# Attention values from rounded high and low parts, and split q and k turned by a product with the identity

## The chip, the cores and the metric

One core of a Trainium2 chip runs the whole program. The metric is the device time of one execution in microseconds, the median over three runs. The engines are TensorE (PE, with its weight loads listed apart as PEld), VectorE (DVE), ScalarE (ACT), GpSimd (POOL) and SyncE (SP), which here issues the DMAs.

## What is computed

One decoder layer over 1024 tokens behind 16 learned meta tokens, all in float32: RMS norm, one input projection, three groups of heads that read the same normalised input (stick-breaking attention, a Mamba-2 state-space group, HGRN2), an output projection, and a squared-ReLU MLP. The change lies in the attention group, 4 heads of 64. Cut to what matters:

```
z = einsum('qd,kd->qk', q, k) * scale           # q, k: RMS-normalised per head
log_w = log_sigmoid(z) + (suffix sum of log_sigmoid(-z) over the keys behind k)
w = where(k < q, exp(log_w), 0)                 # the weights of one block of 128 queries
o = einsum('qk,kd->qd', w, v)                   # the values
out = rmsnorm(o, out_norm)                      # per head
```

## The kernel before

A tile is 128 tokens; tile 0 is the 16 meta tokens, tiles 1 to 8 the sequence. The program goes through these stages: a norm and transposes of the input; `in_gemm` (L366), which projects every tile onto the attention values v (256 columns) and eight decay logits; attention; then eight chunks of state-space and HGRN2 work with the output projection; then the MLP.

Large products are made of float32 numbers split in two: a high part rounded to the type that TensorE takes in a single pass (F32R), written by ACT, and a low part (the number less its high part), written by DVE. A product is then hi*hi + hi*lo + lo*hi, three single-pass matmuls (`gemm_steps`, L185). Plain float32 operands (F32) are also taken by TensorE: the profile then shows two weight loads and two matmuls for each matmul that the program writes.

Attention goes over tiles i = 1 to 8 and in each over heads h = 0 to 3. For each head `scores` (L624), run two heads ahead, forms z in PSUM, takes two sigmoids on ACT, and scans along the keys on DVE. `values` (L652) then takes the weights `sg` in groups of up to four blocks of 128 keys: it transposes them on PE into the one PSUM bank `pb`, copies them to SBUF on ACT (`wT`), and multiplies each block by its tile of v:

```
urgent[0] = A.copy(wT[:, 0:n], pw[:, 0:n])
fill(VGAP)
for j in grp:
    mm(po[:, h * 64:(h + 1) * 64], lhsT=wT[...], rhs=vt[j // 4][:, j % 4, h * 64:(h + 1) * 64], ...)
fill(SGAP); next(ahead, None); fill(HGAP)
```

Here `wT` and `vt` are plain float32, so each block has two loads and two matmuls of 64 columns. There are 48 groups (tiles 1 to 4 have one per head, tiles 5 to 8 two) with 144 blocks in all. After the fourth head a last product adds the meta tokens (`vmb`, L677).

PE's instructions are issued in the order in which the program writes them (`queue`, L112). The orders of DVE, ACT and POOL are made at compile time by a scheduler that simulates the engines; each of them then runs its list in order. `fill(n)` (L757) puts n matmuls of other work between: products of the state-space and HGRN2 projections (bank `mf`), or of the q and k projection of a later tile (bank `mq`). What the fillers have not done by the end of attention is done right after it (L1510), so the total of PE's work doesn't hang on these counts. Each filler product brings work of its own for ACT, DVE and POOL (a convolution of three DVE operations, `split_scaled` of the next weights, and so on).

At the start of each tile `prep_b` (L604) splits the normalised q and k of the next tile into high and low parts side by side, and `stack` (L576) transposes them with `tr`, four 128 by 128 blocks each for q and k: 68 transposes with the tile of meta tokens. At the end of each tile `head_norm` (L565) takes the 256 columns of `po` (one of two buffers of bank `pc`): square on ACT, sum on DVE, a reciprocal root on POOL, a product on DVE, and a store.

Of the kernel before, what the change touches and what calls it, by code (L numbers as in the profile page):

```python
# [8 lines left out]
F32 = mybir.dt.float32  # L9
F32R = mybir.dt.float32r  # L10
BF16 = mybir.dt.bfloat16
U8 = mybir.dt.uint8
AF = mybir.ActivationFunctionType
ALU = mybir.AluOpType

P = 128
D = 1024
# [5 lines left out]
G3 = L + 16  # L23
# [24 lines left out]
ITR = (7, 0)  # L48
PRE = (24, 16, 24, 14, 22, 28)
FILL = (0, 20, 24, 28, 16, 40, 40, 46, 46)  # L50
SGAP, HGAP, VGAP, LOADGAP, BGAP, QGAP, WGAP = 1, 6, 9, 20, 8, 3, 12

BUFS = dict(g1=4, g2=2, g3=8, wsA=1, wsB=1, k4=4, st=3, a1=1, a2=1, a3=1, a4=1, a5=1, qb=1, f4=1, wT=2,
            igt=1, rr=6, ro=2, sm=4, sst=1, fp=2)
# [3 lines left out]
def inner(ap, shape):  # L58

    return ap.rearrange("p (n o) -> p n o", o=1).broadcast_to(shape)  # L60
# [8 lines left out]
def tile_hybrid_block(  # L69
# [34 lines left out]
    V, A, G, SY = (Pinned(e) for e in (nc.vector, nc.scalar, nc.gpsimd, nc.sync))  # L104
# [7 lines left out]
    def queue(i):  # L112
        if fixed[0] and last[0] is not None:
            behind(i, last[0])
        last[0] = i
        return i

    def mm(*a, **k):
        return queue(nc.tensor.matmul(*a, **k))  # L119

    def tr(*a, **k):
        return queue(nc.tensor.transpose(*a, **k))  # L122
# [4 lines left out]
    kto = pool.tile([P, 512], F32, tag="kto", bufs=1, name="kto")  # L127
# [5 lines left out]
    def sb(shape, tag, dt=F32):  # L133
        if tag in ring:
            r = ring[tag]
            r[3] += 1
            at = r[0] + r[3] % r[1] * r[2]
            return cx[:, at:at + shape[0]]
        cnt[0] += 1
        return pool.tile([P] + list(shape), dt, tag=tag, bufs=BUFS[tag], name=f"{tag}_{cnt[0]}")  # L140

    def const(shape, name, dt=F32):
        return pool.tile([P] + list(shape), dt, tag=name, bufs=1, name=name)

    def ps(tag):
        cnt[0] += 1
        return psp.tile([P, 512], F32, tag=tag, bufs=PBUFS[tag], name=f"{tag}_{cnt[0]}")
# [27 lines left out]
    def rms_r(ss, m, n):  # L175

        G.tensor_scalar(ss[:m, :n], ss[:m, :n], 1.0, EPS, ALU.mult, ALU.add)
        rms_last[0] = G.tensor_tensor(ss[:m, :n], ss[:m, :n], mhalf[:m, :n], op=ALU.pow)
# [3 lines left out]
    def rms_tile(tag="rr"):  # L182
        return sb([8], tag)
# [24 lines left out]
    def load_x(i):  # L208
        xt = sb([G3], "g3")[:, 0:D]
        SY.dma_start(xt[:TILES[i][1]], meta if i == 0 else xf[(i - 1) * P:i * P, :])  # L210
        xts[i] = xt
# [40 lines left out]
    ident = const([P], "ident")  # L252
# [4 lines left out]
    pt = ps("pa")  # L257
# [9 lines left out]
    identr, smask = mi[:, 0], mi[:, 1]  # L267
# [85 lines left out]
    def tok_steps(dst, i, w, n0, n1):  # L353
        col, m = TILES[i]
        return gemm_steps(dst, lambda k, a: hx(k, a, col, m), lambda k, a: w[a][:, k, n0:n1])


    vmb = kto[:, 0:256]
    V.memset(vmb, 0.0)
    wv = [sb([KC, NV], t, F32R) for t in ("wsA", "wsB")]  # L360
    vt = [None, None]

    order = [1, 2, 0, 3, 4, 5, 6, 7, 8]
    wq = []
# [1 line left out]
    def in_gemm(n, i):  # L366
        m = TILES[i][1]
        pv = ps(("mq", "pc")[n % 2])
        yield from tok_steps(pv[:m, :NV], i, wv, 0, NV)
        if i:  # L370
            j = (i - 1) // 4
            if vt[j] is None:
                vt[j] = sb([G3], "g3")[:, 0:D].rearrange("p (a b) -> p a b", b=256)
            A.copy(vt[j][:, (i - 1) % 4, :], pv[:m, 0:256])
        else:
            for h in range(4):
                A.copy(vmb[32 * h:32 * h + NM, 64 * h:64 * h + 64], pv[:NM, 64 * h:64 * h + 64])
        V.tensor_copy(dtt[:m, i, :], pv[:m, 256:NV])
        if i == 1:
            load_x(8)  # L380
# [19 lines left out]
    for n, i in enumerate(order):  # L400
        g = in_gemm(n, i)
        if n + 2 < len(order):
            in_norm(order[n + 2])
        for q in range(2):
            take(g, ITR[q] if n else (18, 0)[q])
            if n + 1 < len(order):
                in_tr(order[n + 1], q)
        run(g)
        if n == 2:
            with tc.issue_after(rms_last[0].ins):  # L410
                more_constants()
                masks()
        if n >= 2:
            next(loads, None)
# [142 lines left out]
    def fq_dots():  # L557
        _, p, kg, i0, o0, ni = lateral.pop(0)
        pd = ps("pa")
        for i in range(ni):  # L560
            mm(pd[:, 2 * i:2 * i + 2], lhsT=kg[:, o0 + i * P:o0 + (i + 1) * P], rhs=blk1, start=True, stop=True)
        V.tensor_copy(dtok[:, i0:i0 + ni, p, :], pd[:, 0:2 * ni].rearrange("p (a b) -> p a b", b=2))


    def head_norm(src, m, nh, tag="a1"):  # L565

        nf = sb([8, 64], tag) if tag == "a1" else kto[:, 256:512].rearrange("p (h d) -> p h d", d=64)
        sv = src[:m, :nh * 64].rearrange("p (h d) -> p h d", d=64)
        r = rms_tile("rr" if tag == "a1" else "ro")
        A.activation(nf[:m, :nh], sv, AF.Square, scale=64 ** -0.5)  # L570
        V.reduce_sum(r[:m, :nh], nf[:m, :nh], axis=mybir.AxisListType.X)
        rms_r(r, m, nh)
        V.tensor_tensor(nf[:m, :nh], sv, inner(r[:m, :nh], [m, nh, 64]), op=ALU.mult)
        return nf

    def stack(src, m, tag, bank):  # L576

        hl = sb([4, 2, 64], tag, F32R)
        A.copy(hl[:m, :, 0, :], src)
        V.tensor_tensor(hl[:m, :, 1, :], src, hl[:m, :, 0, :], op=ALU.subtract)  # L580
        pt = ps(bank)
        hf = hl.bitcast(F32)
        for h in range(4):
            tr(pt[:, h * P:h * P + m], hf[:m, h].rearrange("p a d -> p (a d)"), ident[:m, :m])
        return pt

    kT = [sb([G3], "g3", F32R) for _ in range(4)]
# [4 lines left out]
    def prep_a(i):  # L592

        m = TILES[i][1]
        pq = ps("mq" if i else "pc")
        if i == 0:
            yield from tok_steps(pq[:m, :256], i, wq, 256, 512)
            nfs[i] = head_norm(pq, m, 4)
        else:
            yield from tok_steps(pq, i, wq, 0, 512)  # L600
            nfs[i] = head_norm(pq, m, 8)
            G.tensor_tensor(nfs[i][:, 0:4], nfs[i][:, 0:4], outer(wqk, [P, 4, 64]), op=ALU.mult)
# [49 lines left out]
    def values(i, h, po, ahead):  # L652
        sg = sgs.pop((i, h))
        for g0 in range(0, i, 4):
            grp = range(g0, min(i, g0 + 4))
            pw = ps("pb")
            for j in grp:
                tr(pw[:, (j - g0) * P:(j - g0 + 1) * P], sg[:, NM + j * P:NM + (j + 1) * P], ident)
            wT = sb([512], "wT")
            n = len(grp) * P  # L660
            urgent[0] = A.copy(wT[:, 0:n], pw[:, 0:n])
            fill(VGAP)
            for j in grp:
                mm(po[:, h * 64:(h + 1) * 64], lhsT=wT[:, (j - g0) * P:(j - g0 + 1) * P],
                   rhs=vt[j // 4][:, j % 4, h * 64:(h + 1) * 64], start=(h == 0 and j == 0), stop=False)
            fill(SGAP)
            next(ahead, None)
            fill(HGAP)
        for _ in ahead:
            fill(HGAP)  # L670
        if h == 3:
            pw = ps("pb")
            tr(pw[:, 0:P], wm[i % 2].rearrange("p h s -> p (h s)"), ident)
            wT = sb([512], "wT")
            urgent[0] = A.copy(wT[:, 0:P], pw[:, 0:P])
            fill(VGAP)
            mm(po[:, 0:256], lhsT=wT[:, 0:P], rhs=vmb, start=False, stop=True)  # L677


    def z_tile(i):  # L680
# [76 lines left out]
    def fill(n):  # L757
        budget[0] -= n
        while n and fillers:
            if next(fillers[0], True):  # L760
                fillers.pop(0)
                continue
            n -= 1
            nfill[0] += 1
            if side and nfill[0] % LOADGAP == 0 and next(side[0], True):
                side.pop(0)
            if lateral and nfill[0] - lateral[0][0] >= 40:
                fq_dots()
# [29 lines left out]
    sgs, po = {}, None  # L798
# [5 lines left out]
    for n, (i, h) in enumerate(hs):  # L804
        budget[0] = FILL[i]
        if h == 0 and i < 8:
            if i > 1:
                drain(pre[i + 1])
            prep_b(i + 1)
            if i == 7:  # L810
                side.append(load_cols(C_Z, wz))
        if h == 1 and i < 7:
            start_a(i + 2)
        if n == 30:
            side.append(load_wi())
        if h == 0:
            po = ps("pc")
        values(i, h, po, scores(*hs[n + 2]) if n + 2 < len(hs) else iter(()))
        fill(max(0, budget[0]))
        if h == 3:  # L820
            on = head_norm(po, P, 4, "ob")
            SY.dma_start(dr_o[(i - 1) * P:i * P, :], on.rearrange("p h d -> p (h d)"))
# [730 lines left out]
    for i, tag in (("s2", "g2"), ("s3", "g2"), ("22", "g1"), ("s1", "g1")):  # L1553
        t = slab(tag)
# [101 lines left out]
```

## Time and profile before

| | |
|---|---|
| median of 3 runs | 1239.97 us (1239.06 to 1240.15) |
| the profiled execution, its own time | 1240.42 us |
| its span, first to last instruction | 1238.7 us |
| busy share of the span: PE, PEld, DVE, ACT, POOL | 98%, 84%, 71%, 47%, 34% |
| matmuls, and weight loads, in the trace | 6396, 6396 |

All times are in microseconds from the start of the span, unless marked ns. A busy share of PE counts each matmul from its start to the arrival of its last result, and matmuls overlap; what a matmul costs in a stream is the distance between starts, not its duration. Attention runs from 76 to 362 us.

### The profile page before, as it was taken

How to read it: one execution, taken by the hardware profiler on the slowest of the kernel's cores; microseconds unless marked ns; L12 is line 12 of the kernel's file. 1: busy time of each engine (PE TensorE's matmuls, PEld its weight loads, DVE VectorE, ACT ScalarE, POOL GpSimd, SP SyncE). 2: the span in 40 equal slices, each digit the busy share in tenths (PEclk: the TensorE clock that was granted, in tenths of full speed). 3: DMA queues.
4: the chain of work that ended last, by engine and by line, in shares of the span. 5: the costliest groups of instructions: out<-in, count | busy, mean ns of one | idle time of the engine just before them, and what ended most of it. 6: DMA issues, size and time to landing. Idle time of an engine off the chain costs nothing.

```text
span 1238.7 us, 18662 instructions
## 1 busy us (share of the span) xinstructions
PE 1211.4 (98%) x6396; PEld 1038.2 (84%) x6396; DVE 881.1 (71%) x1451; ACT 584.4 (47%) x1237; POOL 424.6 (34%) x498
## 2 busy tenths in 40 slices
PE   8999999999999989999999999999999999999998
PEld 7989999999888768888888888888777888888887
DVE  6777777775323688888456756667998778778777
ACT  6655676664332242333356644454566534344331
POOL 4223322322111467666424646656851000000000
PEclk9999999999999999999999999999999999999999
DMA  6311111233345575462256667767766554554566
GB/s 217 89 41 46 55 40 58 72 95 101 81 125 134 159 227 133 103 128 79 85 162 190 215 210 239 238 225 256 241 212 202 165 162 140 158 158 141 162 197 206
DMA packets 195031, 184.14 MB, mean 149 GB/s; under 512 B 14405, under 2 KB 149853, under 8 KB 194938
## 3 DMA queue, kind: packets, MB, share of 16 engines
q1 hardware_dynamic: 194938, 182.97, 49.3%
q8 instruction: 50, 0.82, 0.3%
q14 instruction: 43, 0.35, 0.1%
HBM read 128.25 MB, written 54.67 MB: 148 GB/s over the span
## 4 chain that ended last, share of the span: by engine, by line
PE 81%; DVE 7%; issue 3%; ACT 3%; POOL 3%; DMA 2%; SPq 0%; DVEq 0%; POOLq 0%; ACTq 0%
PE pa L119 26%; PE mf L119 24%; PE pc L119 17%; PE mq L119 6%; PE pb L119 4%; DVE g L96 2%; DVE k L96 2%; PE pb L122 1%; POOL rr L96 1%; DVE cx L96 1%; PE pa L122 1%; DMA g<-in_w_out_dram 1%; DVE a L96 1%; PE pc L122 1%; POOL cx L96 1%
## 5 line engine op out<-in xcount | busy, mean ns | idle before, releaser
L119 PE MATMUL pa<-g,k 128*128 128x512 f32 x864 | 208.8, 389 | 0.8 <-DVE f L96 0.8
L119 PEld LDWEIGHTS pa<-g,k 128*128 128x128 f32 x864 | 162.0, 188 | 35.2 <-DVE f L96 1.2
L119 PE MATMUL mf<-g,wsA 128*128 128x384 f32 (+2 forms) x624 | 139.3, 357 | 0.0
L119 PE MATMUL mf<-g,wsB 128*128 128x384 f32 (+2 forms) x624 | 137.3, 355 | 0.0
L119 PEld LDWEIGHTS mf<-g,wsA 128*128 128x128 f32 x624 | 103.8, 190 | 6.5 <-DVE g L96 0.3
L119 PEld LDWEIGHTS mf<-g,wsB 128*128 128x128 f32 x624 | 103.4, 189 | 5.8
L96 DVE TENSOR_TENSOR k<-g,k 128x512 fp32r<-128x512 f32 x80 | 81.2, 1016 | 28.7 <-ACT k L96 28.5
L119 PE MATMUL mf<-g,g 128*128 128x512 f32 (+1 forms) x408 | 101.1, 395 | 0.0
L96 ACT CAST g<-cx 128x512 fp32r<-128x512 f32 x80 | 49.5, 619 | 85.5 <-DVE cx L96 58.9
L119 PEld LDWEIGHTS mf<-g,g 128*128 128x128 f32 (+1 forms) x408 | 72.4, 183 | 15.0 <-issue 0.3
L119 PE MATMUL pc<-g,k 128*128 128x512 f32 x336 | 82.5, 389 | 0.0
L96 DVE TENSOR_TENSOR g<-pa,g 128x512 f32<-128x512 f32 (+2 forms) x82 | 54.8, 678 | 36.6 <-PE pa L119 32.2
L96 POOL TENSOR_TENSOR cx<-cx 128x384 f32<-128x384 f32 (+2 forms) x34 | 38.5, 1134 | 118.9 <-ACT cx L96 78.6
L119 PEld LDWEIGHTS pc<-g,k 128*128 128x128 f32 x336 | 63.1, 188 | 13.2
L119 PE MATMUL mf<-g,k 128*128 128x512 f32 x288 | 69.6, 392 | 1.6 <-ACT a L96 1.3
L119 PE MATMUL pa<-g,st 128*128 128x512 f32 x240 | 65.1, 390 | 0.3 <-ACT g L96 0.3
L119 PEld LDWEIGHTS mf<-g,k 128*128 128x128 f32 x288 | 53.6, 188 | 13.4 <-ACT a L96 1.8
L96 DVE TENSOR_TENSOR g<-cx,g 128x512 fp32r<-128x512 f32 x80 | 60.5, 756 | 4.9 <-ACT g L96 3.5
L96 POOL TENSOR_TENSOR g<-g,g 128x512 f32<-128x512 f32 x32 | 45.7, 1437 | 49.8 <-issue 45.5
L96 ACT CAST k<-g 128x512 fp32r<-128x512 f32 x80 | 48.9, 615 | 17.6 <-PE pb L119 9.1
L119 PEld LDWEIGHTS pa<-g,st 128*128 128x128 f32 x240 | 45.0, 188 | 10.1 <-ACT g L96 0.8
L96 DVE SCALAR_TENSOR_TENSOR cx<-cx,cwb 128x384 f32<-128x384 f32 (+1 forms) x72 | 43.5, 605 | 9.2 <-ACT cx L96 8.6
(365 smaller groups left out, 2713.8 us busy)
## 6 DMA issues: line engine op xcount, KB each, us to landing
g<-in_w_up_dram SPq DMA_DIRECT2D x48, 512.0 KB, 4.9
st<-in_w_in_dram SPq DMA_DIRECT2D x51, 256.0 KB, 2.9
cx<-in_w_down_dram SPq DMA_DIRECT2D x48, 256.0 KB, 3.1
wT<-dr_s SPq DMA_DIRECT2D x45, 256.0 KB, 2.9
dr_s<-a SPq DMA_DIRECT2D x40, 256.0 KB, 2.3
g<-in_x_dram SPq DMA_DIRECT2D x16, 512.0 KB, 4.5
dr_s<-st SPq DMA_DIRECT2D x32, 256.0 KB, 2.4
a<-dr_s SPq DMA_DIRECT2D x23, 256.0 KB, 2.9
```

The costliest lines, as they stand in the source:

```text
L96: i = fn(*a, **k)
L119: return queue(nc.tensor.matmul(*a, **k))
L122: return queue(nc.tensor.transpose(*a, **k))
```

## The change

The values of each tile are now kept as a rounded high part and a low part, 64 columns of each side by side for every head (`vt`, four buffers where there were two, each for two tiles). The transposed weights are copied out rounded (`wT`), and a new DVE subtraction writes their low part (`wl`). For each block there is one single-pass matmul of `wT` with 128 columns (v high and v low), and, two filler matmuls later (`LGAP`), one single-pass matmul of `wl` with the 64 columns of v high. `po` holds high and low sums side by side, 128 columns for a head, and `head_norm` first copies the low half out (ACT) and adds the two (DVE). The gap behind the scores, `HGAP`, goes from 6 fillers to 4. In `stack` the transpose becomes a single-pass matmul of the split tile with a rounded identity.

```diff
--- before.py
+++ after.py
@@ -48,7 +48,7 @@
 ITR = (7, 0)
 PRE = (24, 16, 24, 14, 22, 28)
 FILL = (0, 20, 24, 28, 16, 40, 40, 46, 46)
-SGAP, HGAP, VGAP, LOADGAP, BGAP, QGAP, WGAP = 1, 6, 9, 20, 8, 3, 12
+SGAP, HGAP, VGAP, LOADGAP, BGAP, QGAP, WGAP, LGAP = 1, 4, 9, 20, 8, 3, 12, 2
 
 BUFS = dict(g1=4, g2=2, g3=8, wsA=1, wsB=1, k4=4, st=3, a1=1, a2=1, a3=1, a4=1, a5=1, qb=1, f4=1, wT=2,
             igt=1, rr=6, ro=2, sm=4, sst=1, fp=2)
@@ -358,7 +358,8 @@
     vmb = kto[:, 0:256]
     V.memset(vmb, 0.0)
     wv = [sb([KC, NV], t, F32R) for t in ("wsA", "wsB")]
-    vt = [None, None]
+    vt = [const([2, 4, 2, 64], "vx0", F32R), None, const([2, 4, 2, 64], "vx1", F32R), None]
+    osum = const([4, 64], "os")
 
     order = [1, 2, 0, 3, 4, 5, 6, 7, 8]
     wq = []
@@ -368,10 +369,13 @@
         pv = ps(("mq", "pc")[n % 2])
         yield from tok_steps(pv[:m, :NV], i, wv, 0, NV)
         if i:
-            j = (i - 1) // 4
+            j = (i - 1) // 2
             if vt[j] is None:
-                vt[j] = sb([G3], "g3")[:, 0:D].rearrange("p (a b) -> p a b", b=256)
-            A.copy(vt[j][:, (i - 1) % 4, :], pv[:m, 0:256])
+                vt[j] = sb([G3], "g3", F32R)[:, 0:D].rearrange("p (a h t d) -> p a h t d", h=4, t=2, d=64)
+            src = pv[:m, 0:256].rearrange("p (h d) -> p h d", d=64)
+            hi, lo = (vt[j][:, (i - 1) % 2, :, a, :] for a in range(2))
+            A.copy(hi, src)
+            V.tensor_tensor(lo, src, hi, op=ALU.subtract)
         else:
             for h in range(4):
                 A.copy(vmb[32 * h:32 * h + NM, 64 * h:64 * h + 64], pv[:NM, 64 * h:64 * h + 64])
@@ -564,11 +568,18 @@
 
     def head_norm(src, m, nh, tag="a1"):
 
-        nf = sb([8, 64], tag) if tag == "a1" else kto[:, 256:512].rearrange("p (h d) -> p h d", d=64)
-        sv = src[:m, :nh * 64].rearrange("p (h d) -> p h d", d=64)
         r = rms_tile("rr" if tag == "a1" else "ro")
-        A.activation(nf[:m, :nh], sv, AF.Square, scale=64 ** -0.5)
-        V.reduce_sum(r[:m, :nh], nf[:m, :nh], axis=mybir.AxisListType.X)
+        if tag == "a1":
+            nf = sq = sb([8, 64], tag)
+            sv = src[:m, :nh * 64].rearrange("p (h d) -> p h d", d=64)
+        else:
+            sv = nf = kto[:, 256:512].rearrange("p (h d) -> p h d", d=64)
+            hl = src.rearrange("p (h t d) -> p h t d", t=2, d=64)
+            sq = osum
+            A.copy(osum, hl[:, :, 1, :])
+            V.tensor_tensor(nf, hl[:, :, 0, :], osum, op=ALU.add)
+        A.activation(sq[:m, :nh], sv, AF.Square, scale=64 ** -0.5)
+        V.reduce_sum(r[:m, :nh], sq[:m, :nh], axis=mybir.AxisListType.X)
         rms_r(r, m, nh)
         V.tensor_tensor(nf[:m, :nh], sv, inner(r[:m, :nh], [m, nh, 64]), op=ALU.mult)
         return nf
@@ -579,9 +590,9 @@
         A.copy(hl[:m, :, 0, :], src)
         V.tensor_tensor(hl[:m, :, 1, :], src, hl[:m, :, 0, :], op=ALU.subtract)
         pt = ps(bank)
-        hf = hl.bitcast(F32)
         for h in range(4):
-            tr(pt[:, h * P:h * P + m], hf[:m, h].rearrange("p a d -> p (a d)"), ident[:m, :m])
+            mm(pt[:, h * P:h * P + m], lhsT=hl[:m, h].rearrange("p a d -> p (a d)"), rhs=identr[:m, :m], start=True,
+               stop=True)
         return pt
 
     kT = [sb([G3], "g3", F32R) for _ in range(4)]
@@ -656,13 +667,18 @@
             pw = ps("pb")
             for j in grp:
                 tr(pw[:, (j - g0) * P:(j - g0 + 1) * P], sg[:, NM + j * P:NM + (j + 1) * P], ident)
-            wT = sb([512], "wT")
+            wT, wl = sb([512], "wT", F32R), sb([512], "fp", F32R)
             n = len(grp) * P
             urgent[0] = A.copy(wT[:, 0:n], pw[:, 0:n])
+            V.tensor_tensor(wl[:, 0:n], pw[:, 0:n], wT[:, 0:n], op=ALU.subtract)
             fill(VGAP)
             for j in grp:
-                mm(po[:, h * 64:(h + 1) * 64], lhsT=wT[:, (j - g0) * P:(j - g0 + 1) * P],
-                   rhs=vt[j // 4][:, j % 4, h * 64:(h + 1) * 64], start=(h == 0 and j == 0), stop=False)
+                mm(po[:, h * P:(h + 1) * P], lhsT=wT[:, (j - g0) * P:(j - g0 + 1) * P],
+                   rhs=vt[j // 2][:, j % 2, h].rearrange("p t d -> p (t d)"), start=(h == 0 and j == 0), stop=False)
+            fill(LGAP)
+            for j in grp:
+                mm(po[:, h * P:h * P + 64], lhsT=wl[:, (j - g0) * P:(j - g0 + 1) * P],
+                   rhs=vt[j // 2][:, j % 2, h, 0, :], start=False, stop=False)
             fill(SGAP)
             next(ahead, None)
             fill(HGAP)
@@ -674,7 +690,8 @@
             wT = sb([512], "wT")
             urgent[0] = A.copy(wT[:, 0:P], pw[:, 0:P])
             fill(VGAP)
-            mm(po[:, 0:256], lhsT=wT[:, 0:P], rhs=vmb, start=False, stop=True)
+            mm(po.rearrange("p (h t d) -> p h t d", t=2, d=64)[:, :, 0, :], lhsT=wT[:, 0:P], rhs=vmb, start=False,
+               stop=True)
 
 
     def z_tile(i):
```

## Rows read from the trace of the kernel before

**Rows 1.** The page: busy time by engine, and the chain that ended last, by engine.

```profile
PE 1211.4 (98%) x6396; PEld 1038.2 (84%) x6396; DVE 881.1 (71%) x1451; ACT 584.4 (47%) x1237; POOL 424.6 (34%) x498
...
PE 81%; DVE 7%; issue 3%; ACT 3%; POOL 3%; DMA 2%; SPq 0%; DVEq 0%; POOLq 0%; ACTq 0%
```

**Rows 2.** Busy us (count) of PE, PEld, DVE, ACT, POOL by stage; PE clock, DMA.

```profile
76.00:181.00 105.00, 102.77 (x665) 96.86 (x666) 80.83 (x176) 65.65 (x186) 31.22 (x38) 1.00 0.17 50
181.00:300.00 119.00, 119.00 (x800) 115.85 (x799) 85.74 (x152) 75.06 (x191) 35.23 (x34) 1.00 0.28 82
300.00:362.00 62.00, 62.00 (x344) 53.86 (x343) 21.86 (x29) 21.71 (x45) 11.03 (x22) 1.00 0.38 96
```

**Rows 3.** Timeline around one group of four value blocks: start, us, engine, instructions.

```profile
250.17 1.00 PE L119 MATMUL pc<-g,wT 128*128 128x64 f32 x8
...
250.98 0.42 PE L119 MATMUL mf<-g,wsA 128*128 128x384 f32 x1
...
251.24 0.57 PE L119 MATMUL pa<-g,a 128*128 128x456 f32 x2
...
251.65 1.21 PE L119 MATMUL mf<-g,wsA 128*128 128x384 f32 x6
...
252.70 0.38 PE L122 MATMUL pb<-ident,g 128*128 128x128 f32 x2
```

**Rows 4.** Timeline, weight loads of rounded operands one behind the other (76.97 on).

```profile
76.69 0.35 PE L122 MATMUL pa<-ident,k 40*128 40x40 f32 x3
...
76.97 0.30 PEld L119 LDWEIGHTS pa<-g,a 128*128 128x128 f32 x2
...
77.19 0.19 PEld L119 LDWEIGHTS pa<-mi 128*128 128x128 f32 x1
...
77.30 0.43 PEld L119 LDWEIGHTS mf<-g,wsB 128*128 128x128 f32 x3
```

**Rows 5.** Timeline of eight transposes of split k and q, and the next.

```profile
259.20 0.60 PE L122 MATMUL pc<-ident,a 128*128 128x128 f32 x4
...
259.64 0.60 PE L122 MATMUL mq<-ident,a 128*128 128x128 f32 x4
...
260.07 0.60 PE L122 MATMUL pb<-ident,k 128*128 128x128 f32 x4
```

**Rows 6.** Groups by shape, 76 to 362 us: count, busy us, mean ns, idle before.

```profile
L122 PE MATMUL pa<-ident,k 40*128 40x40 f32 x8 | 0.7, 228 | 0.0
...
L96 DVE TENSOR_TENSOR a<-mq,rr 128x512 f32<-128x512 f32 x7 | 4.8, 692 | 2.5 <-POOL rr L96 2.4
...
L96 DVE TENSOR_TENSOR kto<-pc,ro 128x256 f32<-128x256 f32 x7 | 3.0, 423 | 2.5 <-POOL ro L96 2.3
...
L96 DVE TENSOR_TENSOR cx<-mf,cx 128x384 f32<-128x384 f32 x4 | 2.2, 550 | 0.0
...
L96 DVE TENSOR_TENSOR k<-k,k 128x127 f32<-128x127 f32 x3 | 0.8, 280 | 0.0
```

**Rows 7.** Timeline of the group whose copy DVE's work follows worst.

```profile
240.26 2.44 DVE L96 TENSOR_TENSOR_SCAN g<-g 128x784 f32<-128x784 f32 x1
240.45 0.59 ACT L96 COPY wT<-pb 128x512 f32<-128x512 f32 x1 [0.55 <-PE pb L122]
...
241.37 1.00 PE L119 MATMUL pc<-g,wT 128*128 128x64 f32 x8
```

**Rows 8.** Timeline of the last group.

```profile
354.30 0.59 ACT L96 COPY wT<-pb 128x512 f32<-128x512 f32 x1 [0.59 <-PE pb L122]
...
356.12 1.00 PE L119 MATMUL pc<-g,wT 128*128 128x64 f32 x8
```

**Rows 9.** Timeline at the border of tiles 2 and 3.

```profile
131.64 0.49 ACT L96 COPY wT<-pb 128x384 f32<-128x384 f32 x1
131.78 0.68 DVE L96 CAST qb<-mq 64x512 fp32r<-64x512 f32 x1 [1.34 <-ACT qb L96]
...
132.18 0.88 PE L119 MATMUL pc<-g,wT 128*128 128x64 f32 x6 [1.21 <-ACT wT L96]
```

## The prediction

> **What bounds the kernel now.** I read the page first: PE is busy 98% of the span and carries 81% of the chain that ended last [rows 1]. Then the stages: over the whole of attention, 76 to 362 us, TensorE's granted clock is full, and from 181 us on PE has no idle time at all; before that it idles 2.2 of 105 us, while DVE is busy 77% of that stretch, 72% of the next one and 35% of the last [rows 2]. So a change in attention is worth what it takes from or adds to PE's own stream, plus any wait that it puts into that stream. Fillers don't make a wait free: PE runs in program order, so a product that waits holds up the fillers behind it, and all of them must be done before the end.
>
> The timeline says what a short matmul costs in the stream. The reader is to look at distances between starts. Six fillers of 384 columns take from 251.65 to 252.70, 0.175 us each. From the first value matmul at 250.17 to the start of the scores at 251.24 is 1.07 us, in which stand eight value matmuls and one filler: (1.07 - 0.175) / 8 = 0.112 us for each matmul of 64 columns [rows 3].
>
> **The change, part by part.**
>
> Value products. Before: 144 blocks of two plain float32 passes, 288 matmuls of 64 columns at 0.112 us, 32.2 us. After: 144 matmuls of 128 columns and 144 of 64, all single-pass, again 288 matmuls with 288 weight loads. The columns fall, but what sets the 0.112 us? The row for rounded operands is where loads stand behind one another: two loads at 76.97 last 0.30 us together and the one load that follows shows 0.19, so they start 0.11 apart; the next start at 77.19 and 77.30, 0.11 again [rows 4]. These serve matmuls of 144 and 128 columns, the plain float32 ones above serve 64: the distance is that of the load, whatever the columns and the type. So I take 0.112 us for the new matmuls as well, and the edit is worth nothing on PE: 288 x 0.112 before and after. Splitting a group in two parts with two fillers between doesn't alter this, since the first load of a part hides under a filler and the load of the filler behind it shows.
>
> The Trainium skill says the same of the load (TensorE: Matmul & The Clock Gate, section LDWEIGHTS): its time is the number of its columns over 1.2 GHz, 107 ns for 128, whatever the matmul does; the rows agree with 0.11 us. The same page (section on fast weight load) states a rule that would speak otherwise: a fast load is on for 128 weights that are not FP32, about twice as fast as measured there; by it the rounded operands would load in about half the time, an estimate from that page. No run here shows it: the rounded loads stand 0.11 us apart.
>
> Transposes. Before: four of k, four of q, then the next four start at 259.20, 259.64 and 260.07, 0.109 us each [rows 5]. After: 68 single-pass products with loads of 0.11 us: 68 x 0.002 = 0.1 us more. Three transposes of 40 columns at 76.69 start 0.06 us apart ((0.35 - 0.23) / 2, with 0.23 us for one) [rows 4, 6], so a transpose's own load is the shorter one and it is the columns that set the 0.109; an edge where a transpose follows a product may gain 0.05 us, some 0.4 in all eight tiles. I count the two as 0.
>
> DVE's new work. The low part of the weights is one subtraction a group, read from PSUM. By width the nearest rows are 0.28 us for 128 columns, 0.42 for 256, 0.55 for 384 and 0.69 for 512 [rows 6]. Of the 48 groups 24 are of four blocks and eight each of one, two and three: 24 x 0.69 + 8 x (0.28 + 0.42 + 0.55) = 26.6 us. The low parts of v add 8 x 0.42 and the sums in `head_norm` 8 x 0.42: 33 us in all, plus 3 us of ACT copies. DVE has the room: 33 us against 286 - 188 = 98 idle ones in attention [rows 2]. So the work itself is hidden; what counts is when it is done.
>
> The wait for `wl`. Behind this subtraction on DVE's list stand the scans and the convolutions; what waits for it on PE is the second part of the group and every filler after it. PE gets there n x 0.112 + 2 x 0.175 us after the first value product of a group of n blocks. The subtraction can start when ACT's copy and DVE's running instruction are done, lasts its width's time, and takes 0.15 us to be seen (an estimate: three times the 0.05 us between the end of a copy at 132.13 and the product at 132.18 that waited for it [rows 9]). In the last group: copy done at 354.89, product at 356.12, second part due at 356.12 + 0.45 + 0.35 = 356.92, `wl` there at 354.89 + 0.69 + 0.15 = 355.73: no wait [rows 8]. In the worst: copy done at 241.04, but a scan holds DVE until 242.70, so `wl` is there at 243.54, while PE is due at 241.37 + 0.80 = 242.17: a wait of 1.37 us [rows 7]. I did this sum for all 48 groups of the trace, the first with its product at 88.40, the last at 356.12. With nothing but the running instruction ahead of the subtraction, eight groups wait, 3.9 us together. If the instruction that follows it back to back on DVE is also ahead, 15 groups wait, 9.3 us; with two such, 22 groups, 16.4 us. The lower bound is 0 (the scheduler puts every subtraction first and moves the scans). I take 5 us: the subtraction is ready as soon as the copy is, while the filler work in front of it on DVE is mostly waiting for ACT, so the first case is the nearer one; but some backlog there is, DVE being busy three quarters of the time up to 300 us.
>
> The tile borders. The sum of the halves, 0.42 us [rows 6], comes to DVE just when PE and ACT go through `prep_b` and the first group of the next tile. There the margin is thin: between tiles 2 and 3 the copy ends at 132.13 and PE has waited 1.21 us for it by 132.18, with a cast on DVE until 132.46 [rows 9]. By the same sum with 0.42 us more ahead of `wl`, the seven borders wait 1.2 us more. The bounds are 0 and 7 x 0.42 = 2.9 us; I take 1.2.
>
> The start. The low part of v stands ahead of the copy of the decay logits on DVE; in the last tile of `in_gemm` this heads a chain that PE waits for later. At most 0.42 us [rows 6], taken as 0.4. The earlier release of `po` (its last reader is now the sum, not the product behind POOL's root) and the gap of 4 + 2 in place of 6 fillers I count at nothing: the fillers per group remain 16, and the scores, two heads ahead, come 0.35 us later in the group. If that cover were gone the first sigmoid would be late by this much.
>
> Sum: 0 (products) + 0 (transposes) + 5 (waits for `wl`) + 1.2 (borders) + 0.4 (start) = 6.6 us. On the profiled execution's own 1240.42 us that is 1247.0; it stands 0.45 above the median of 1239.97, so the median to expect is 1246.6, rounded to 1246.5. A difference under 0.2%, 2.5 us, is about what a measurement here can't tell from none.
>
> **The rivals.**
>
> Hidden after all: the waits stay under 2.5 us, since the nine fillers ahead of each product leave most copies done over 0.5 us early; about 1241 us. For it: from 300 us on no group waits even with queued work ahead. Against: eight groups are late at the best. Chance 0.20.
>
> A backlog: two queued instructions stand ahead of each subtraction. Then the waits are 16.4 us, with the borders and the start 18.0: 1258 us. For it: DVE is three quarters busy up to 300 us, and its list is fixed at compile time, so a scan or a convolution that waits can stand before the subtraction. Against: a quarter of idle time means that queues are mostly short. Chance 0.12.
>
> PE becomes cheaper: the loads of the new single-pass products take less than those of plain float32. The nearest row of a shorter load is that of the small transposes, 0.06 us [rows 4]. At that price, in the value groups and in `stack`, PE would save 144 x (2 x 0.112 - 2 x 0.062) + 68 x (0.109 - 0.062) = 14.4 + 3.2 = 17.6 us, against 6.6 of waits: 1229 us. It decides for faster from a saving of 9.1 us, that is below 0.087 us for each of 356 products. Against it speak the rounded loads at 0.11 us [rows 4]. The skill's fast load, above, is this rival by another reason. Chance 0.10.
>
> That the waits of before shrink, as the 1.21 us between tiles 2 and 3, when the orders of ACT and DVE are made anew: the trace has about 3 us of these in attention; they outweigh the new ones only if nearly all `wl` are on time. About 1237 us; chance 0.04.
>
> **How the numbers follow.** My forecast, slower by 3 to 12 us, has 0.54. Slower by over 0.2% is that and the backlog: 0.66. The same: 0.20. Faster: 0.10 + 0.04 = 0.14. The range goes from 1237, where it leaves out the cheaper PE, to 1257, where it cuts the backlog in its middle: left out are some 0.10 + 0.06. The likeliest case's own range is 1243 to 1252.
>
> **What the profile after would show.** Right: 288 value matmuls in two forms, single-pass, still 0.11 us apart in the group; PE waiting for DVE at the second part, mostly up to 300 us and behind scans; DVE about 33 us busier. Wrong: value products closer than 0.09 us, or loads that don't show between them (the forecast then falls on the side of faster); no wait of PE for `wl` (the same); or waits in more than 20 groups (the backlog). A longer chain from the ends of tiles into `wT` would show as waits of PE for ACT at the first product of a tile.

## The result, and the profile after

The changed kernel takes 1249.84 us (median of 4 runs, 1249.29 to 1251.03), the kernel before 1240.06 us beside it: a ratio of 1.0074, 95% interval 1.0062 to 1.0087. It is slower by about 9 us. The span of the profiled execution goes from 1238.7 to 1248.0 us.

The page of the changed kernel, busy time by engine and the chain that ended last; it answers to [rows 1]:

```profile
PE 1216.3 (97%) x6396; PEld 1039.0 (83%) x6396; DVE 910.4 (73%) x1515; ACT 587.6 (47%) x1245; POOL 422.0 (34%) x498
...
PE 77%; DVE 11%; ACT 4%; issue 3%; POOL 3%; DMA 2%; DVEq 0%; SPq 0%; POOLq 0%; ACTq 0%
```

The counts are the first thing to see: as many matmuls and weight loads as before, with the same load time in all. DVE has 64 instructions and 29 us more, and its share of the chain has gone from 7 to 11%. The same stages as in [rows 2], with the same columns:

```profile
76.00:181.00 105.00, 101.86 (x653) 94.68 (x653) 87.83 (x194) 67.13 (x187) 30.43 (x38) 1.00 0.16 47
181.00:300.00 119.00, 114.08 (x748) 107.61 (x747) 93.05 (x171) 72.74 (x189) 32.04 (x33) 1.00 0.25 74
300.00:362.00 62.00, 61.92 (x354) 54.92 (x353) 30.45 (x40) 21.61 (x48) 10.10 (x16) 1.00 0.34 91
```

From 181 to 300 us PE was never idle before; now it is, 4.9 us by this count, and it gets through 748 matmuls where there were 800. The weights of the meta tokens are transposed for the last time at 369.3 instead of 358.6 us (a group's first and last start stand behind the durations; of the kernel before first, then of the changed one):

```profile
L122 PE MATMUL pb<-ident,wm x8: 270/274/306, 103.0 to 358.6; 128*128 128x128 f32 x8
```

```profile
L122 PE MATMUL pb<-ident,wm x8: 270/274/306, 103.6 to 369.3; 128*128 128x128 f32 x8
```

So the loss lies in attention. Who waited for whom there (76 to 372 us of the changed kernel; total us, times, longest):

```profile
PEld pc L119 <- DVE fp L96: 12.0, 18, 1.3
PE pc L119 <- DVE fp L96: 6.7, 10, 1.0
PEld pc L119 <- ACT wT L96: 1.7, 3, 0.8
```

`fp` is the tag in which `wl` lies. The loader (PEld) idles 12.0 us in 18 places for the subtraction; a part of each is hidden under the filler in front. Measured on the matmuls (the distance from the last filler's start to the first second product, less what that filler takes), the 18 waits are 9.55 us. One of them, in the timeline:

```profile
255.82 0.59 ACT L96 CAST wT<-pb 128x512 fp32r<-128x512 f32 x1 [1.17 <-PE pb L122]
...
256.34 1.08 DVE L96 TENSOR_TENSOR k<-k,k 128x895 f32<-128x895 f32 x1
...
257.24 0.30 PEld L119 LDWEIGHTS pc<-g,wT 128*128 128x128 f32 x2
257.30 0.39 PE L119 MATMUL pc<-g,wT 128*128 128x128 f32 x2
257.34 1.00 DVE L96 TENSOR_TENSOR cx<-cx 128x272 f32<-128x272 f32 x1
257.46 0.30 PEld L119 LDWEIGHTS mf<-g,wsA 128*128 128x128 f32 x2
257.52 0.56 PE L119 MATMUL mf<-g,wsA 128*128 128x384 f32 x2
...
258.27 0.68 DVE L96 TENSOR_TENSOR fp<-pb,wT 128x512 fp32r<-128x512 f32 x1
258.99 0.30 PEld L119 LDWEIGHTS pc<-vx,fp 128*128 128x128 f32 x2 [1.23 <-DVE fp L96]
259.00 0.41 PE L119 MATMUL pc<-vx,fp 128*128 128x64 f32 x2 [0.91 <-DVE fp L96]
```

The copy is done at 256.41. DVE then finishes a product over 895 keys and runs one of 272 columns for a filler before it comes to the subtraction, which starts 1.86 us late. PE is through the two fillers at 257.93 (the second starts at 257.755 and takes 0.175 in the stream) and stands until 259.00. The rounded products show the predicted distance: loads at 257.24 and 257.35 (0.30 less one load's 0.19), then 257.46.

### The profile page after: what moved, and what is told of

It reads as the page before. It is cut to its first block, busy times and chain, and to the rows that moved or that the text cites. A ratio compares the mean times of both kernels' runs of the same rounds, so it can differ in the third digit from the quotient of the medians.

```text
span 1248.0 us, 18722 instructions
## 1 busy us (share of the span) xinstructions
PE 1216.3 (97%) x6396; PEld 1039.0 (83%) x6396; DVE 910.4 (73%) x1515; ACT 587.6 (47%) x1245; POOL 422.0 (34%) x498
## 4 chain that ended last, share of the span: by engine, by line
PE 77%; DVE 11%; ACT 4%; issue 3%; POOL 3%; DMA 2%; DVEq 0%; SPq 0%; POOLq 0%; ACTq 0%
PE pa L119 26%; PE mf L119 22%; PE pc L119 17%; PE mq L119 6%; PE pb L119 3%; DVE g L96 3%; DVE k L96 2%; DVE cx L96 2%; POOL rr L96 2%; PE pb L122 1%; DVE a L96 1%; PE pa L122 1%; DMA g<-in_w_out_dram 1%; ACT k L96 1%; POOL cx L96 1%
## 5 line engine op out<-in xcount | busy, mean ns | idle before, releaser
L119 PE MATMUL mf<-g,wsB 128*128 128x384 f32 (+2 forms) x624 | 140.8, 357 | 0.0
L119 PEld LDWEIGHTS pa<-g,st 128*128 128x128 f32 x240 | 45.0, 188 | 10.1 <-ACT g L96 0.7
L119 PE MATMUL mq<-g,g 128*128 128x512 f32 x192 | 50.8, 404 | 0.4 <-DVE a L96 0.4
```

## Experiments

All ratios are to the kernel before, run on the same chip beside each.

**1. No wait, all the work (e1).** The second products read `wT`:

```diff
-                mm(po[:, h * P:h * P + 64], lhsT=wl[:, (j - g0) * P:(j - g0 + 1) * P],
+                mm(po[:, h * P:h * P + 64], lhsT=wT[:, (j - g0) * P:(j - g0 + 1) * P],
```

> The changed kernel with one edit: the second products take the rounded weights again in place of their low part, so that PE has the same stream of 288 value matmuls but no product waits for the DVE subtraction, which is still done and then read by nothing (the output lacks the low parts of the weights). Theory A, PE's wait for the subtraction is the loss: the changed kernel's trace has 18 such waits of 9.55 us in all, so this one comes to 1249.8 - 9.5 = 1240.3 us. Theory B, DVE's 33 us of added work delays the scans and the other chains: most of the loss stays, 1247 to 1250 us. Theory C, the longer ends of the tiles and the other edits: stays too, over 1247 us.

1240.16 us, ratio 0.9992 (0.9983 to 1.0000). The output then lacks the low part of the weights. With the wait alone taken out, all of the loss is gone, DVE's added work, the sums at the tile borders and the split of v being still there. Theories B and C fall.

**2. No subtraction either (e2).** Beside the edit of e1:

```diff
-            V.tensor_tensor(wl[:, 0:n], pw[:, 0:n], wT[:, 0:n], op=ALU.subtract)
```

> As the run before, and the subtraction is left out altogether (48 DVE instructions, 26.6 us by their widths). Theory A: 1240.3 us, no difference from the run before within 1 us. Theory B: only now the loss is gone, 1240 to 1242 us here while the run before stays near 1249. Theory C: still over 1247 us.

1242.36 us, ratio 1.0013 (1.0004 to 1.0022). Taking 48 instructions from DVE gains nothing; the run came out 0.2% above e1, which no theory expected. Where the time lies is seen in the granted clock. Both kernels wait for the state-space work between 432 and 437 us, PE idle for 3.6 us in e1 and 3.5 in e2, and the clock then falls to its lower level (0.50, 1.2 GHz); in e2 it stays there longer. The stretch behind, in e1 and then in e2 (columns as in [rows 2]):

```profile
440.00:448.00 8.00, 6.64 (x35) 5.20 (x33) 7.29 (x12) 0.03 (x1) 5.03 (x8) 1.00 0.44 147
```

```profile
440.00:448.00 8.00, 6.73 (x28) 5.20 (x27) 6.26 (x10) 0.99 (x2) 4.63 (x7) 0.84 0.48 157
```

35 matmuls against 28, and spans of 1238.0 and 1239.8 us. The mean granted clock of e2's runs is 0.995 to 0.998 in ten of 11, that of e1's is 0.998 or 0.999 in eight of 11. At the same mean clock, 0.997, e2's four runs took 1241.35 to 1243.28 us and e1's three 1240.84 to 1241.48, so over the runs the clock is not shown to be all of it. Why it recovers later in e2 stays open.

**3. More fillers in front of the second part (e3).** Complete computation.

```diff
-SGAP, HGAP, VGAP, LOADGAP, BGAP, QGAP, WGAP, LGAP = 1, 4, 9, 20, 8, 3, 12, 2
+SGAP, HGAP, VGAP, LOADGAP, BGAP, QGAP, WGAP, LGAP = 1, 0, 9, 20, 8, 3, 12, 6
```

> The changed kernel with six fillers instead of two between the first and the second part of a group and none behind the scores, 16 in all as before; the computation is complete. Four more fillers of 0.175 us give the subtraction 0.7 us more. Theory A: of the 18 waits in the changed kernel's trace what is over 0.7 us is left, 2.1 us in seven groups, so 1249.8 - 7.4 = 1242.4 us, 1241 to 1244 with the scores moved. Theory B and C: no change, 1248 to 1251 us.

1246.87 us, ratio 1.0043 (1.0030 to 1.0056): about half of the expected gain. The waits of this run:

```profile
PEld pc L119 <- DVE fp L96: 6.2, 10, 1.3
PE pc L119 <- DVE fp L96: 3.5, 7, 1.1
```

The waits are halved and the loss falls by two fifths (0.0074 to 0.0043), so the mechanism holds; but they should have fallen to a quarter. In this run the subtraction starts up to 2.4 us behind its copy, where the changed kernel's latest was 1.9: other DVE work had moved in front of it. Extra distance can't be counted as if the order on the other engine stayed.

**4. The new `stack` alone, in the kernel before (e4).**

```diff
-            tr(pt[:, h * P:h * P + m], hf[:m, h].rearrange("p a d -> p (a d)"), ident[:m, :m])
+            mm(pt[:, h * P:h * P + m], lhsT=hl[:m, h].rearrange("p a d -> p (a d)"), rhs=identr[:m, :m], start=True,
+               stop=True)
```

> The kernel before with the new stack alone: the transposes of split q and k are single-pass products with the rounded identity. If a rounded load costs 0.111 us and the transposes of before 0.109, no change: 1240.1 us within 0.5. If the product is priced by its columns (128 at 2.4 GHz, 0.06 us), 68 x 0.05 = 3.4 us faster: 1236.7 us.

1241.42 us, ratio 0.9999 (0.9990 to 1.0009): the transposes are worth nothing, as the load's price says.

**5. More columns (e5).** The second products take both halves of v.

```diff
-                mm(po[:, h * P:h * P + 64], lhsT=wl[...], rhs=vt[j // 2][:, j % 2, h, 0, :], ...)
+                mm(po[:, h * P:(h + 1) * P], lhsT=wl[...],
+                   rhs=vt[j // 2][:, j % 2, h].rearrange("p t d -> p (t d)"), ...)
```

> The changed kernel with 128 columns instead of 64 in the second products: the low part of the weights times both parts of the values (one term more than the product of three; the output is complete). If the weight load sets the 0.111 us of a short product, the columns are free: 1249.8 us within 1, ratio 1.007 to the kernel before. If columns are paid (64 more at 2.4 GHz, 27 ns, 144 times): 3.8 us slower, 1253.7 us.

1250.64 us, ratio 1.0078 (1.0065 to 1.0090), where the changed kernel has 1.0074: the 64 columns more are free.

**6. Without the second products (e6).** Loop and subtraction left out, the filler count kept.

```diff
-            V.tensor_tensor(wl[:, 0:n], pw[:, 0:n], wT[:, 0:n], op=ALU.subtract)
...
-            for j in grp:
-                mm(po[:, h * P:h * P + 64], lhsT=wl[:, (j - g0) * P:(j - g0 + 1) * P], ...)
```

> The changed kernel without the second products and the subtraction (the low parts of the weights are left out of the output): 144 matmuls of 64 columns fewer, and no wait for DVE. By the load's price of 0.111 us: 16.0 us below the run without the waits, whose ratio to the kernel before is 0.9992: 1224 us, ratio 0.987. By the price of the columns alone, 144 x 0.027 = 3.8 us: 1236 us, ratio 0.996.

1226.25 us, ratio 0.9879 (0.9866 to 0.9893). Against e1 that is 0.0113 x 1241 = 14.0 us for 144 matmuls, 0.097 us each: near the load's 0.111, far from the 0.028 that 64 columns take by the 0.227 us of 512 (measured in e11). Where 2 us are lacking, the stage 372 to 420 us shows an idle PE, 2.2 us (e1 has none there), its longest wait being one of 0.9 us for ACT:

```profile
372.00:420.00 48.00, 45.79 (x244) 38.36 (x244) 29.79 (x50) 14.27 (x34) 18.30 (x32) 1.00 0.55 162
```

**7. The second part one group late (e7).** Complete computation.

```diff
...
             fill(VGAP)
+            second()
             for j in grp:
                 mm(po[:, h * P:(h + 1) * P], lhsT=wT[...], ...)
+            waiting.append((po, h, g0, grp, wl))
             fill(LGAP)
-            for j in grp:
-                mm(po[:, h * P:h * P + 64], lhsT=wl[...], ...)
```

> The changed kernel with the second products put off by one group: they stand behind the fillers of the next group, in front of its first products; fillers and products are the same in number, the computation is complete. The subtraction then has a whole group more. Theory A: no wait for it is left, the time is that of the kernel before, 1240 us, ratio 0.999 to 1.001. Theory B, DVE's load as such: still over 1247 us.

1239.10 us, ratio 0.9983 (0.9974 to 0.9992). `second` issues the second products of the group before. No wait of a product for `wl` is left in its list, and the loss is gone with the same work on every engine. That the change as such, freed of its wait, comes out 0.2% ahead is at the edge of what is measured; nothing in the trace was tied to it.

**8. The values as the loaded operand (e8).** If loads are what short products cost, there should be fewer. The pair of v's halves (128 columns) is loaded, and the high and low weights pass side by side; the turned sums are folded and turned back later by plain float32 products with `fold`, two identities on top of each other. Complete computation.

```diff
+                mm(pt[:, h % 2 * 256:h % 2 * 256 + 256], lhsT=vt[j // 2][:, j % 2, h].rearrange("p t d -> p (t d)"),
+                   rhs=w[(j - grp[0]) // 2][:, (j - grp[0]) % 2].rearrange("p a q -> p (a q)"), ...)
...
+                A.copy(sums, pv[:, :, 1, :])
+                V.tensor_tensor(folded[:, h - 1:h + 1, :], pv[:, :, 0, :], sums, op=ALU.add)
...
+            mm(po[:, h * 64:(h + 1) * 64], lhsT=folded[:, h, :], rhs=fold, start=(h == 0), stop=False)
```

> The values as the loaded operand instead: high and low parts of v side by side are loaded once for each block and head, and the high and low weights pass in one matmul of 256 columns; the sums, turned, are added by ACT and DVE and turned back by plain float32 products with two identities on top of each other, put off into the next tile. 144 products at the 0.117 us of a 256-column matmul in the trace of before (16.8 us) take the place of 288 at 0.111 (32.0 us), and 32 products back cost two loads each, 7.1 us. If the load is the price: 8 us faster than the kernel before, 1232 us, ratio 0.9935, if no new wait comes in. If the columns were the price, 256 against 128 and 64: slower than the kernel before, over 1245 us.

1236.89 us, ratio 0.9968 (0.9956 to 0.9981): faster than both kernels, by half of what the loads promise. The trace shows a new wait, of the next transposes (`pb`, one bank) for the last of two subtractions that read the bank; by distances 6.1 us in 11 places, more than the 4 us that lack. The largest:

```profile
242.72 0.94 DVE L96 TENSOR_TENSOR g<-g,g 128x767 f32<-128x767 f32 x1
...
243.93 0.41 DVE L96 TENSOR_TENSOR fp<-pb,fp 128x256 fp32r<-128x256 f32 x1
...
244.48 0.41 PE L122 MATMUL pb<-ident,k 128*128 128x128 f32 x2 [1.62 <-DVE fp L96]
```

**9, 10. One copy and one subtraction for a group (e9), and fillers shared out anew (e10).** A wide operand tile had to find room, so the scratch rows of two tags were made narrower.

```diff
-G3 = L + 16
-K4 = L + 48
+G3 = L + 4
+K4 = L
...
+            n, w = len(grp), sb([4, 2, P], "wT", F32R)
+            urgent[0] = A.copy(w[:, 0:n, 0, :], pv[:, 0:n, :])
+            V.tensor_tensor(w[:, 0:n, 1, :], pv[:, 0:n, :], w[:, 0:n, 0, :], op=ALU.subtract)
```

and for e10, beside that,

```diff
-SGAP, HGAP, VGAP, LOADGAP, BGAP, QGAP, WGAP = 1, 6, 9, 20, 8, 3, 12
+SGAP, HGAP, VGAP, LOADGAP, BGAP, QGAP, WGAP = 1, 8, 9, 20, 8, 3, 12
```

> The turned products with one copy and one subtraction for a group of four blocks instead of two of each (the operand tile made wide enough, some scratch rows narrower). In the run before it PE lost 6.1 us in 11 waits of the next transposes for the bank of the transposes, which the last subtraction frees. Theory A (a DVE subtraction that runs late is paid wherever PE waits for its outcome, here the bank): with 32 subtractions and copies fewer most of these go, 1232 to 1235 us, ratio 0.993 to 0.996. If the bank is not the cause: no change, ratio 0.997.

> The same with eight fillers instead of six behind the scores: two more between the products of a group and the next transposes, taken from those at the end of a head, so that the fillers remain about the same in number. Theory A: the bank's remaining waits fall by up to 0.35 us each, 0 to 3 us faster than the run beside it. If fillers are the cost: slower by the 0.176 us of each that is added and not taken away elsewhere, under 2 us.

e9: 1240.22 us, ratio 0.9997 (0.9987 to 1.0006); e10: 1248.55 us, ratio 1.0055 (1.0038 to 1.0072). By the time both expectations failed. By the trace of e9 the first did not: the waits for the bank fell from 6.1 to 0.8 us, and attention ended 8 us sooner than in the kernel before, at 350.7:

```profile
L122 PE MATMUL pb<-ident,wm x8: 271/272/306, 104.5 to 350.7; 128*128 128x128 f32 x8
```

The MLP gave it back. Its matmuls that read `k`, in the timeline of e9:

```profile
801.68 5.70 PE L119 MATMUL pa<-g,k 128*128 128x512 f32 x24
807.22 0.40 PE L119 MATMUL pc<-wsA,k 128*128 128x512 f32 x1
```

24 of them take from 801.68 to 807.22, 0.231 us each. The first `pa<-g,k` starts at 699.0 and the end of the span is at 1237.4, 538.4 us, where the kernel before has 531.3 (1238.7 - 707.4; the kernel before first, then e9):

```profile
L119 PE MATMUL pa<-g,k x864: 387/389/497, 707.4 to 1224.7; 128*128 128x512 f32 x173
```

```profile
L119 PE MATMUL pa<-g,k x864: 388/393/498, 699.0 to 1223.2; 128*128 128x512 f32 x173
```

e10, the same kernel with eight fillers for six, has a span 10.1 us longer than e9. Its trace shows four losses. The first transpose for the meta tokens starts 3.0 us later than in e9 (107.5 for 104.5): PE waits 0.9 us longer for its first weights (the product at 9.81 starts at 8.92 in e9), and then the clock falls, with 48 matmuls from 10 to 20 us where e9 has 68. In attention PE waits twice for the bank, 3.0 us in all (e9: once, 0.2), and behind the longer of these waits the clock falls again. The windows from 10 to 20 us and around that wait, and the wait in the timeline:

```profile
10.00:20.00 10.00, 8.53 (x48) 7.89 (x48) 6.28 (x14) 6.73 (x17) 2.65 (x6) 0.66 0.88 298
...
279.00:280.00 1.00, 0.00 (x0) 0.00 (x0) 1.00 (x3) 0.86 (x2) 0.54 (x1) 1.00 0.84 309
...
281.00:282.00 1.00, 1.00 (x8) 1.00 (x8) 0.87 (x3) 0.72 (x2) 0.00 (x0) 0.80 0.86 217
282.00:283.00 1.00, 1.00 (x7) 1.00 (x6) 0.50 (x1) 0.00 (x0) 0.00 (x0) 0.50 0.82 307
283.00:284.00 1.00, 1.00 (x6) 1.00 (x6) 0.00 (x0) 0.00 (x0) 0.00 (x0) 0.50 0.50 74
284.00:285.00 1.00, 1.00 (x5) 0.90 (x5) 0.00 (x0) 0.10 (x1) 0.18 (x1) 0.50 0.50 188
285.00:286.00 1.00, 1.00 (x7) 1.00 (x7) 0.52 (x1) 1.00 (x3) 0.34 (x1) 1.00 0.00 0
```

```profile
280.03 0.55 PE L122 MATMUL pb<-ident,k 128*128 128x128 f32 x3 [2.36 <-DVE wT L96]
```

The fall at 281 us costs 0.2 + 3 x 0.5 = 1.7 us, if PE's work there goes with the clock. And PE waits longer for the folded sums (`sst`), first in e9, then in e10:

```profile
PE pc L119 <- DVE sst L96: 0.6, 1, 0.6
```

```profile
PE pc L119 <- DVE sst L96: 3.0, 2, 2.0
```

Start, waits for the bank, this fall and the sums come to 3.0 + 3.0 - 0.2 + 1.7 + 3.0 - 0.6 = 9.9 of the 10.1 us. Of e10's six runs five had a mean granted clock of 0.994 to 0.997 and took 1247.4 us or more; the one at 1.000 took 1243.57. e9's runs at 1.000 took 1238.67 to 1239.69. So of the 8.3 us between the medians some 4 are left at equal clocks, and the rest goes with the clock. The loss at the start can't be put down to the two fillers: e7's profiled execution, without them, has the same one, with the clock at 0.66 and 50 matmuls from 10 to 20 us.

```profile
10.00:20.00 10.00, 8.58 (x50) 8.13 (x51) 6.28 (x15) 6.73 (x16) 2.66 (x6) 0.66 0.87 305
```

There too PE waits longer for its first weights (1.25 us; e10 1.45, e9 0.51). Why these come late in some executions stays open.

**11, 12. The rows wide again (e11), and the kernel before with narrow ones (e12).** e11 is e9 with `K4 = L + 48`, three small constants having moved into one buffer of the tag `fp` to make room; e12 is the kernel before with

```diff
-K4 = L + 48
+K4 = L
```

> The turned products with one copy and one subtraction for each group, and the scratch rows of the tag k4 as wide as in the kernel before (1088 elements instead of 1040); the room comes from two small tiles put into one. In the run with narrow rows attention ended 8 us sooner than in the kernel before, but the MLP took 538.4 us instead of 531, its 512-column matmuls that read k4 standing 231 ns apart instead of 227. Theory A with the rows as the cause of that loss: 1232 us, ratio 0.993 (0.991 to 0.995). If the loss came from the turned products or their order: ratio 0.9997 as before.

> The kernel before with one edit: the rows of the tag k4 are 1040 elements wide instead of 1088. If the width of the rows (and where they then lie) slows the MLP's matmuls by 4 ns each: 1247 to 1249 us, ratio 1.005 to 1.007, and 231 ns between the matmuls that read k4. If not: 1241 us, ratio 1.000.

e11: 1232.90 us, ratio 0.9930 (0.9914 to 0.9947). e12: 1249.75 us, ratio 1.0067 (1.0053 to 1.0082). Both as expected if the width of the rows is the cause. The same stretch in e11 (24 matmuls in 5.44 us, 0.227 each), and the matmuls from 800 to 860 us, 267 in the kernel before and 262 in e12:

```profile
800.45 5.60 PE L119 MATMUL pa<-g,k 128*128 128x512 f32 x24
805.89 0.39 PE L119 MATMUL pc<-wsA,k 128*128 128x512 f32 x1
```

```profile
800.00:860.00 60.00, 60.00 (x267) 49.67 (x266) 39.33 (x53) 29.07 (x51) 39.46 (x28) 1.00 0.71 239
```

```profile
800.00:860.00 60.00, 60.00 (x262) 48.72 (x261) 37.23 (x53) 27.68 (x48) 38.73 (x27) 1.00 0.69 232
```

From the first `pa<-g,k` to the end the MLP takes 531.4 us in e11 (from 699.8) and 538.5 in e12 (from 709.4): 7 us hang on this edit. e11 is the fastest of the kernels that compute everything: 0.7% ahead of the kernel before and 1.4% (0.9930 / 1.0074) ahead of the changed one. Its value products, two for the load of two, in the trace:

```profile
224.03 0.40 PE L119 MATMUL pc<-wT,vx 128*128 128x256 f32 x2
224.26 0.40 PE L119 MATMUL pc<-wT,g 128*128 128x256 f32 x2
224.50 0.34 PE L119 MATMUL mf<-g,wsB 128*128 128x384 f32 x1
```

Four blocks in 0.47 us, 0.117 each, where the kernel before paid two loads, 0.224.

## Why the prediction was right, and where it was off

The forecast was slower, 1246.5 us, by the waits for `wl`; measured are 1249.84 us and that mechanism. Point by point:

- *The products are worth nothing on PE.* Right. The rounded loads stand 0.11 us apart in the trace after, e5 shows that 64 more columns are free, e6 that a matmul costs nearly a load, e4 the same for `stack`. The rival of cheaper loads is out, and with it the fast load that the Trainium skill's page (TensorE: Matmul & The Clock Gate, fast weight load) would give to rounded operands: no run shows one.
- *DVE's new work is hidden as such.* Right: DVE is 29 us busier (33 were forecast), e1 keeps it at 0.9992, e2 without it is no faster.
- *The waits for `wl`, taken as 5 us, and 1.2 us more at the tile borders.* Right in mechanism and place (all 18 end before 295 us), off in size: both terms are the same wait, 6.2 us together, and it measured 9.55. The step that failed is the choice between the two sums, 3.9 with only the running instruction ahead and 9.3 with one more. The reason given, that the subtraction is ready first and so comes first, doesn't hold: in the wait shown above work for a filler ran between the product over the keys and the subtraction. In 14 of the 18 waits something started on DVE between the end of the copy and the subtraction: one instruction in eight, two to four in six. So the second sum came near in its total, but one queued instruction is not the rule (10 of its 15 groups are among the 18), and that it fits so well is in part luck. Nor did the waits stand mostly behind scans: in two of the 18 a scan was running when the copy ended.
- *The borders by themselves.* The first groups of tiles 2 to 7 hold six of the 18 waits and 3.3 of the 9.55 us; the same sums by group give 0.5 (first) and 1.7 us (second) for them on the trace of before. In four of the six the reduction in `head_norm` ran just ahead of the subtraction, and in a fifth the new sum was running when the copy ended. How much the new sum adds was not tested by itself: e1 keeps it, but there no product waits for `wl`. One of them, between tiles 3 and 4 (0.92 us):

```profile
160.74 0.68 DVE L96 CAST a<-mq 64x512 fp32r<-64x512 f32 x1
...
161.45 0.42 DVE L96 TENSOR_REDUCE ro<-os 128x4 f32<-128x256 f32 x1
...
161.79 0.68 DVE L96 TENSOR_TENSOR fp<-pb,wT 128x512 fp32r<-128x512 f32 x1
...
162.52 0.41 PE L119 MATMUL pc<-vx,fp 128*128 128x64 f32 x2 [0.75 <-DVE fp L96]
```

- *The start, 0.4 us.* Not seen: e1 keeps the edit and stands at the kernel before's time. But 0.4 us is 0.0003 of it, less than its interval (0.9983 to 1.0000) can tell.
- *The sum.* 6.6 us were forecast. The median moved by 9.8, the ratio says 9.2, and the waits on PE are 9.55. The waits, 6.2 forecast and 9.55 measured, account for what the sum fell short; the median came out 3.3 us above the 1246.5.
- *The backlog rival* (22 groups, 16.4 us) was too dark, *hidden after all* too light. *That the waits of before shrink* came true in small: PE's waits for `wT` in attention went from 1.8 to 0.5 us.

## What to carry to other kernels

Price a short matmul by the distance between starts in the trace and ask what sets it before counting columns: where it is the load, doubling the columns cost nothing (e5) and halving the loads gained 0.7% (e11). An operand that gets a second producer on a busier engine brings that engine's queue into PE's stream; give it a whole group of distance (e7) rather than a few fillers (e3), and look at what else the late instruction frees, such as a bank (e8). When a gain fails to arrive, compare the stages behind the edit too (e9's was lost 350 us later), and the granted clock behind each wait (e10).

## What the runs showed of the hardware

The 512-column matmuls of the MLP that read tiles of the tag `k4` stand 231 ns apart with rows of 1040 elements and 227 with 1088 (e9 against e11), which makes 7 us over the MLP (538.4 and 538.5 us in e9 and e12, 531.4 and 531.3 in e11 and the kernel before). The whole of e12, with 2 us more ahead of the MLP, is 0.67% slower. That the edit of the width does it is shown; whether it is the rows' stride, where the tiles begin or what lies beside them is open. e11 keeps the other tag's rows narrow, so those are not the cause.

A wait of PE can cost more than itself. In e10 the 2.36 us that ended at 280.03 were followed by a fall of the granted clock to its lower level (0.50, 1.2 GHz), 1.7 us more, though PE was busy again by then; in e2 the clock is lower than in e1 by 0.05 at 432 to 440 us and by 0.16 at 440 to 448, 8 x 0.21 = 1.7 of the 1.8 us between the spans. A wait of 1.76 us in e9, which ended at 13.85 us, had no such fall behind it. At the start of the program the three profiled executions in which PE waits 1.2 us or more for its first weights (e5, e7, e10: 1.23, 1.25, 1.45 us) show a lower clock from 10 to 20 us (0.83, 0.66, 0.66); the other eleven wait 0.38 to 0.51 us there and keep the full clock. So differences of 0.2% and less (e2, e7) are not read here as effects of an edit.
